# Hybrid encoder trunk on one core: four of sixteen k-tiles of two products as plain float32, and two tiles padded

## The chip, the cores and the metric

The kernel runs on one core of one Trainium2 chip. The metric is the device time of one execution in microseconds (us); before the change it is 3089.78 us, the median of three runs (3088.32 to 3091.51).

## What is computed

The trunk has two layers on 256 tokens of 2048 features, in float32. What matters of the reference:

```python
for i in range(DEPTH):                          # 2
    hn = rmsnorm(h, mix_norm[i])
    if i == 0:
        mix = conformer_conv_module(hn, ...)    # u = hn @ w_pw1 (2048 -> 4096), a * sigmoid(gate),
                                                # 31-tap depthwise convolution, layernorm, silu, @ w_pw2
    else:
        mix = gated_deltanet_bidir(hn, ...)     # proj = hn @ w_in (2048 -> 12416), short convolution,
                                                # two scans over 32 value heads, gated norm, @ w_out
    h = h + mix
    h = h + swiglu_ffn(rmsnorm(h, ffn_norm[i]), w_gate_up[i], w_down[i])   # hidden size 5632
return rmsnorm(h, final_norm)
```

## The kernel before, in words

Features lie on the 128 partitions and the 256 tokens along the free axis. Every product holds a block of 128 output features as its stationary weights and runs over k-tiles of 128 input features. `products` (L163) takes the weights of a column block in chunks of eight k-tiles: one DMA of 512 KB from SP's queue into a tile `raw` (L149), of which there are three. A chunk is cut into groups of four k-tiles.

The matmuls take float32r operands, which hold a float32 less exactly. So `halves` (L152) makes of each group of weights a high part `hi` (a cast on ScalarE, L159) and a low part `lo` (a subtraction on VectorE, L160) that float32r holds exactly, with four buffers of each (`HI`). The activations are split in the same way: `norm_tile` (L213) writes the high part of a k-tile to the left half of a tile `xs` (L219) and the low part to the right half (L220); the residual stream is multiplied by the norm's weights there, and the token's factor comes behind the product. Two forms of product use them:

- *wide* (L184, L185, L187): per k-tile a matmul of 512 columns, `hi` with both halves of the activations, and one of 256 columns, `lo` with the high half. This form is used in pw2 (on `y`), in both SwiGLU stages (`gu` on `xs`, `dn` on `hs`) and in wout (on `ys`).
- *not wide* (L189, L190, L191): three matmuls of 256 columns per k-tile, all added up in one half of a PSUM bank. This form is used in the first product of the convolution module (pw1, 32 blocks of 128 features) and in the input product of the DeltaNet (win, 97 blocks), both with 16 k-tiles on `xs`.

The stages follow each other: pw1 with the taps of the depthwise convolution, on GpSimd (L344), VectorE (L354) and, for four blocks, TensorE (L340); layer norm and pw2; SwiGLU 0; the DeltaNet; wout; SwiGLU 1; the final norm. In the DeltaNet VectorE also works on the short convolution (L594), the inverses (L690 to L730) and the heads (L810), and GpSimd on the masks and inverses. The order of the instructions on each engine is set when the program is built: a scheduler with a model of the times places them, and priorities lift some (`halves` by 800, the heads and the front of the DeltaNet by 550). Each engine works through its own list in that order, and SP's queue too: a load of weights waits there until its `raw` tile is free, and what stands behind it waits as well.

Tiles lie one behind another in a partition, in the order in which the pools are opened: constants (with `par_sb`), activations (`xs`), weights (`raw`, `hi`, `lo`), small tiles, and then the pools of the stages. The starts are multiples of 32 bytes.

Of the kernel before, what the change touches and what calls it, by code (L numbers as in the profile page):

```python
# [7 lines left out]
F32 = mybir.dt.float32  # L8
F32R = mybir.dt.float32r
AF = mybir.ActivationFunctionType  # L10
# [3 lines left out]
P = 128  # L14
# [11 lines left out]
# PSUM banks  # L26
# [11 lines left out]
# taps of the depthwise convolution that GpSimd adds, by feature block  # L38
NPOOL = [15] * 12 + [14, 13, 6, 5]

# columns of the packed per-feature parameters
# [11 lines left out]
# columns of the packed constants  # L53
# [13 lines left out]
def fv(ap, off, *dims):  # L67
    """A view of a tile by an offset and [stride, count] pairs over its free elements."""
    return bass.AP(ap.tensor, ap.offset + off, [list(ap.ap[0]), *[list(d) for d in dims]])


class Trunk:
    def __init__(self, ctx, tc, x, par, cst, pw1, pw2, win, wout, gu, dn, out):
# [15 lines left out]
        self.par = self.cp.tile([P, NRES], F32, name="par_sb")  # L89
# [3 lines left out]
    def new_h(self):  # L93
        """The residual stream on chip, in a pool of its own."""
# [8 lines left out]
    def load_first(self, srcs):  # L103
        """The input and the first weights, in the order in which they are needed."""
# [34 lines left out]

    def raw_tile(self):  # L140
        """A chunk of weights; every other one from a phase that has room for more of them."""
# [4 lines left out]
    def raw_weights(self, src, k0, n):  # L146
        """n k-tiles of one column block."""
# [4 lines left out]
    def halves(self, raw, i, n, pool=None):  # L152
        """k-tiles i to i + n as a high and a low part that float32r holds exactly."""
# [9 lines left out]
    def products(self, srcs, kt, acts, wide=False, tags=("lin",), pool=None, order=None):  # L163
        """Blocks of 128 output features, k-tile by k-tile; acts: float32r tiles [P, hi | lo].

        order: of the k-tiles, within each CS of them."""
# [3 lines left out]
        for k0 in range(0, kt, CK):  # L170
            n = min(CK, kt - k0)
            raws = self.ahead.pop(0) if self.ahead else [self.raw_weights(s, k0, n) for s in srcs]
            for i in range(0, n, CS):
                m = min(CS, n - i)
                ws = [self.halves(r, i, m, pool) for r in raws]
# [31 lines left out]

    def norm_begin(self):
# [4 lines left out]
    def norm_tile(self, k, wname, wi, prep=True, first=None):  # L213
# [3 lines left out]
        if prep:  # L217
# [26 lines left out]
    def warm(self, func, after):  # L244
        """Loads a function's table on ScalarE, ahead of its use."""
        t = self.sp.tile([P, 1], F32, tag="warm", bufs=1, name=self.nm("warm"))
        self.nc.scalar.activation(t, after[:, :1], func)
# [10 lines left out]
    def norm_end(self):  # L258
        """The factor is traced behind the next product, whose result is the first to need it."""
# [4 lines left out]

    def conv_module(self, next_norm):
# [3 lines left out]
        with tc.tile_pool(name="conv", bufs=1, reuse_waits="tile") as cv:  # L269
            self.norm_begin()  # L270
# [26 lines left out]
            def add(key, t, n, last):  # L297
                """Sums over the channels, added up in PSUM."""
# [658 lines left out]
```

## Time and profile before

| | |
|---|---|
| median of three runs | 3089.78 us |
| lowest and highest run | 3088.32, 3091.51 us |
| span of the profiled execution | 3092.0 us |
| TensorE matmul busy | 2859.3 us (92%), x18122 |
| VectorE busy | 2332.2 us (75%), x3735 |
| ScalarE busy | 1695.6 us (55%), x3449 |
| GpSimd busy | 1009.9 us (33%), x1047 |
| mean granted clock of TensorE | 0.970 |
| stages, by the first and last of their work, us | pw1 5 to 314, pw2 348 to 440, SwiGLU 0 440 to 1183, DeltaNet 1183 to 2132, wout 2132 to 2336, SwiGLU 1 2336 to 3078 |

The profile is of one execution. Its span is the time from the first to the last instruction; no time of its own is given for that execution beside the span, which is 2.2 us above the median and 0.5 us above the slowest run. PE is TensorE's matmul, PEld its weight load, DVE VectorE, ACT ScalarE, POOL GpSimd and SP the engine that issues most DMAs. The end of a matmul is modelled, and matmuls overlap: how fast they follow each other is read from their starts. The granted clock is TensorE's, as a share of 2.4 GHz.

### The profile page before, as it was taken

The numbers are of one execution on the slowest core, as the hardware profiler recorded it, in microseconds if no ns is written. First come the engines' busy times: TensorE is split into PE (matmuls) and PEld (weight loads), VectorE is DVE, ScalarE is ACT, GpSimd is POOL, SyncE is SP. The second block draws the span as 40 slices with busy tenths as digits, with TensorE's granted clock in tenths as the row PEclk, the third lists the DMA queues.
The fourth block names the chain that finished last, engine by engine and source line by source line (L and its number), as shares of the span: only waits on it lengthen the run. The fifth ranks groups of instructions, "written<-read, shape, count | busy, mean of one in ns | idle before, by whom it ended". The sixth has DMA issues, their size and how long they took to land. (4 is left out here: it accounts for less than half of the span.)

```text
span 3092.0 us, 50294 instructions
## 1 busy us (share of the span) xinstructions
PE 2859.3 (92%) x18122; PEld 2566.7 (83%) x18122; DVE 2332.2 (75%) x3735; ACT 1695.6 (55%) x3449; POOL 1009.9 (33%) x1047
## 2 busy tenths in 40 slices
PE   7778799999999999878888889888999999999998
PEld 6777688888888889877888888888888888888887
DVE  8999876666666667899899997985766666666555
ACT  6665555555555445654665456554545555555443
POOL 6777420000000111566667766562110000000111
PEclk9999899999999999999999999999999999999999
DMA  4333266555556665543544445456666555556664
GB/s 164 121 112 103 89 202 189 188 185 188 186 186 193 197 200 166 181 150 115 164 155 149 137 144 166 129 158 200 192 189 209 185 187 188 185 187 184 192 190 141
DMA packets 163866, 521.38 MB, mean 169 GB/s; under 512 B 18240, under 2 KB 34944, under 8 KB 163616
## 3 DMA queue, kind: packets, MB, share of 16 engines
q1 hardware_dynamic: 162320, 516.86, 52.7%
q8 instruction: 142, 2.33, 0.3%
q10 hardware_dynamic: 1296, 1.30, 0.1%
q14 instruction: 108, 0.88, 0.1%
HBM read 497.02 MB, written 21.07 MB: 168 GB/s over the span
## 5 line engine op out<-in xcount | busy, mean ns | idle before, releaser
L160 DVE TENSOR_TENSOR lo<-raw,hi 128x512 fp32r<-128x512 f32 x1764 | 1384.7, 788 | 644.6 <-ACT hi L159 638.3
L159 ACT CAST hi<-raw 128x512 fp32r<-128x512 f32 x1764 | 1085.9, 619 | 935.4 <-PE acc L185 692.8
L185 PE MATMUL acc<-xs,hi 128*128 128x512 f32 x2816 | 982.0, 398 | 0.6 <-ACT hi L159 0.6
L184 PE MATMUL acc<-xs,lo 128*128 128x256 f32 x2640 | 742.3, 281 | 0.0
L191 PE MATMUL acc<-xs,lo 128*128 128x256 f32 x2064 | 620.1, 302 | 96.4 <-DVE lo L160 95.6
L189 PE MATMUL acc<-xs,hi 128*128 128x256 f32 x2064 | 606.1, 295 | 31.1 <-ACT hi L159 18.9
L185 PEld LDWEIGHTS acc<-xs,hi 128*128 128x128 f32 x2816 | 517.7, 188 | 116.4 <-ACT hi L159 0.9
L190 PE MATMUL acc<-xs,hi 128*128 128x256 f32 x2064 | 605.2, 294 | 0.8 <-DVE xs L220 0.7
L191 PEld LDWEIGHTS acc<-xs,lo 128*128 128x128 f32 x2064 | 410.9, 200 | 128.8 <-DVE lo L160 123.0
L184 PEld LDWEIGHTS acc<-xs,lo 128*128 128x128 f32 x2640 | 499.0, 189 | 6.8
L185 PE MATMUL acc<-hs,hi 128*128 128x512 f32 x1408 | 486.8, 391 | 0.0
L189 PEld LDWEIGHTS acc<-xs,hi 128*128 128x128 f32 x2064 | 413.8, 201 | 37.1 <-ACT hi L159 21.1
L190 PEld LDWEIGHTS acc<-xs,hi 128*128 128x128 f32 x2064 | 413.9, 201 | 6.1 <-issue 4.3
L184 PE MATMUL acc<-hs,lo 128*128 128x256 f32 x1376 | 388.0, 282 | 0.0
L421 POOL TENSOR_TENSOR tg<-tg,rstd 128x256 f32<-128x256 f32 x88 | 65.0, 738 | 920.9 <-ACT tg L420 920.9
L185 PEld LDWEIGHTS acc<-hs,hi 128*128 128x128 f32 x1408 | 262.2, 188 | 53.4
L184 PEld LDWEIGHTS acc<-hs,lo 128*128 128x128 f32 x1376 | 259.9, 189 | 1.6
L230 POOL TENSOR_TENSOR sq<-h 128x256 f32<-128x256 f32 x59 | 55.0, 931 | 562.7 <-DVE h L432 383.9
L344 POOL TENSOR_TENSOR a<-a,m 128x256 f32<-128x256 f32 x218 | 196.3, 908 | 56.1 <-ACT m L343 45.8
L594 DVE SCALAR_TENSOR_TENSOR u<-t,par_sb,u 128x254 f32<-128x254 f32 (+1 forms) x256 | 178.8, 704 | 3.4 <-ACT u L590 2.2
L185 PE MATMUL acc<-ys,hi 128*128 128x512 f32 x512 | 177.8, 396 | 1.1 <-DVE ys L204 1.1
L184 PE MATMUL acc<-ys,lo 128*128 128x256 f32 x496 | 137.9, 286 | 1.8 <-ACT ys L203 1.6
(226 smaller groups left out, 3503.9 us busy)
## 6 DMA issues: line engine op xcount, KB each, us to landing
raw<-in_gu SPq DMA_DIRECT2D x352, 512.0 KB, 4.6
raw<-in_win SPq DMA_DIRECT2D x194, 512.0 KB, 3.8
raw<-in_dn SPq DMA_DIRECT2D x160, 512.0 KB, 3.6
raw<-in_pw SPq DMA_DIRECT2D x94, 512.0 KB, 3.3
raw<-in_wout SPq DMA_DIRECT2D x64, 512.0 KB, 3.7
a_d<-am SPq DMA_DIRECT2D x32, 384.0 KB, 2.7
ar<-a_d SPq DMA_DIRECT2D x32, 384.0 KB, 4.8
raw<-in_dn SPq DMA_DIRECT2D x32, 256.0 KB, 4.3
```

Source lines behind the costliest of these rows:

```text
L159: nc.scalar.copy(hi, r)
L160: nc.vector.tensor_tensor(lo, r, hi.bitcast(F32), op=ALU.subtract)
L184: nc.tensor.matmul(acc[:, S:], lo, a[:, :S], start=False, stop=False)
L185: nc.tensor.matmul(acc, hi, a, start=first, stop=last)
L189: nc.tensor.matmul(acc[:, :S], hi, a[:, :S], start=first, stop=False)
L190: nc.tensor.matmul(acc[:, :S], hi, a[:, S:], start=False, stop=False)
L191: nc.tensor.matmul(acc[:, :S], lo, a[:, :S], start=False, stop=last)
L230: (nc.vector if last else nc.gpsimd).tensor_tensor(sq, h, h, op=ALU.mult)
L344: nc.gpsimd.tensor_tensor(acc, acc, m, op=ALU.add)
L421: nc.gpsimd.tensor_tensor(tg, tg, rstd, op=ALU.mult)
L594: nc.vector.scalar_tensor_tensor(u[:, lo:hi], t[:, lo + s : hi + s], w(i), u[:, lo:hi], op0=ALU.mult, op1=ALU.add)
```

## The change

In the products on the norm's output, a norm may now name groups of k-tiles as *plain*: group 0 for pw1 (`PLAIN1`), group 3 for win (`PLAIN2`, passed by SwiGLU 0, whose last norm feeds the DeltaNet). For such a group `norm_tile` writes the product of the residual stream with the norm's weights as float32, without a low part, and `products` multiplies the loaded weights as they are: one plain float32 matmul of 256 columns per k-tile in place of three, with `raw` itself as the stationary operand and no cast and no subtraction. Besides, `par_sb` is padded from 499 to 512 columns and `warm` from 1 to 32. Comments are blanked as well; with the added lines, what stands behind them moves down by up to 16.

```diff
+PLAIN1, PLAIN2 = (0,), (3,)
...
-        self.par = self.cp.tile([P, NRES], F32, name="par_sb")
+        self.par = self.cp.tile([P, -(-NRES // 32) * 32], F32, name="par_sb")[:, :NRES]
...
                 m = min(CS, n - i)
+                if acts[order[k0 + i]].dtype == F32:
+                    for x in range(k0 + i, k0 + i + m):
+                        for acc, r in zip(accs, raws):
+                            nc.tensor.matmul(acc[:, :S], r[:, (x - k0) * P : (x - k0 + 1) * P], acts[order[x]],
+                                             start=(x == 0), stop=(x == kt - 1))
+                    continue
                 ws = [self.halves(r, i, m, pool) for r in raws]
...
-    def norm_begin(self):
+    def norm_begin(self, plain=()):
+        self.plain = plain
...
-        if prep:
+        if prep and k // CS in self.plain:
+            xs = self.xp.tile([P, 2 * S], F32, tag=f"xs{k}", name=self.nm(f"xp{k}"))[:, :S]
+            nc.scalar.activation(xs, h, AF.Copy, scale=w)
+            self.xs[k] = xs
+        elif prep:
...
-        t = self.sp.tile([P, 1], F32, tag="warm", bufs=1, name=self.nm("warm"))
-        self.nc.scalar.activation(t, after[:, :1], func)
+        t = self.sp.tile([P, 32], F32, tag="warm", bufs=1, name=self.nm("warm"))
+        self.nc.scalar.activation(t[:, :1], after[:, :1], func)
...
-            self.norm_begin()
+            self.norm_begin(PLAIN1)
...
-            self.norm_begin()
+            self.norm_begin(PLAIN2 if prep else ())
```

How this stands in the built programs. On TensorE, at the end of the third block of the DeltaNet's input product, the kernel before has (a row is line, operation, result, moving operand and weights, size; the numbers tell buffers apart):

```order
L189 MATMUL acc_2650_12874<-xs14_2565_12403,hi_2659_12927 128x256
L190 MATMUL acc_2650_12874<-xs14_2565_12403,hi_2659_12927 128x256
L191 MATMUL acc_2650_12874<-xs14_2565_12403,lo_2660_12928 128x256
L189 MATMUL acc_2650_12874<-xs15_2596_12557,hi_2659_12927 128x256
L190 MATMUL acc_2650_12874<-xs15_2596_12557,hi_2659_12927 128x256
L191 MATMUL acc_2650_12874<-xs15_2596_12557,lo_2660_12928 128x256
L189 MATMUL acc_2666_12958<-xs0_2132_10249,hi_2668_12961 128x256
```

and the changed kernel, at the end of that block:

```order
L199 MATMUL acc_2582_12458<-xs11_2408_11553,hi_2589_12495 128x256
L200 MATMUL acc_2582_12458<-xs11_2408_11553,hi_2589_12495 128x256
L201 MATMUL acc_2582_12458<-xs11_2408_11553,lo_2590_12496 128x256
L182 MATMUL acc_2582_12458<-xp12_2439_11707,raw_2588_12493 128x256
L182 MATMUL acc_2582_12458<-xp13_2470_11860,raw_2588_12493 128x256
L182 MATMUL acc_2582_12458<-xp14_2501_12013,raw_2588_12493 128x256
L182 MATMUL acc_2582_12458<-xp15_2532_12166,raw_2588_12493 128x256
L199 MATMUL acc_2596_12530<-xs0_2068_9861,hi_2598_12533 128x256
```

The last four k-tiles are four rows in place of twelve, and they read `raw` instead of `hi` and `lo`. On VectorE, where the same blocks' weights are split at the start of the DeltaNet, the kernel before has four subtractions for the third block (those from raw_2651 and raw_2656):

```order
L160 TENSOR_TENSOR lo_2653_12878<-raw_2651_12875,hi_2652_12877 128x512
L255 RECIPROCAL rstd_2619_12735<-rstd_2619_12735 128x256
L160 TENSOR_TENSOR lo_2655_12894<-raw_2651_12875,hi_2654_12893 128x512
L535 TENSOR_TENSOR t_2620_12738<-acc_2607_12664,rstd_2619_12735 128x256
L160 TENSOR_TENSOR lo_2658_12912<-raw_2656_12909,hi_2657_12911 128x512
L589 TENSOR_TENSOR t_2645_12859<-acc_2634_12790,rstd_2619_12735 128x256
L536 TENSOR_SCALAR t_2620_12738<-t_2620_12738,cst_sb_70,par_sb_71 128x256
L160 TENSOR_TENSOR lo_2660_12928<-raw_2656_12909,hi_2659_12927 128x512
```

and the changed kernel three (from raw_2583 and raw_2588):

```order
L163 TENSOR_TENSOR lo_2585_12462<-raw_2583_12459,hi_2584_12461 128x512
L163 TENSOR_TENSOR lo_2587_12478<-raw_2583_12459,hi_2586_12477 128x512
L271 RECIPROCAL rstd_2553_12331<-rstd_2553_12331 128x256
L163 TENSOR_TENSOR lo_2590_12496<-raw_2588_12493,hi_2589_12495 128x512
L551 TENSOR_TENSOR t_2554_12334<-acc_2543_12272,rstd_2553_12331 128x256
L552 TENSOR_SCALAR t_2554_12334<-t_2554_12334,cst_sb_70,par_sb_71 128x256
L163 TENSOR_TENSOR lo_2599_12534<-raw_2597_12531,hi_2598_12533 128x512
```

The subtraction for the fourth group is gone, and the next one in the list is that of the next block. In all, the program has 1635 subtractions of weights for 1764 before, as many casts less, 56 subtractions of `xs` for 64, and 516 plain matmuls in place of 1548.

## Rows read from the trace of the kernel before

**Rows 1.** The page: the span and part 1, busy us, share, number of instructions.
```profile
span 3092.0 us, 50294 instructions
...
PE 2859.3 (92%) x18122; PEld 2566.7 (83%) x18122; DVE 2332.2 (75%) x3735; ACT 1695.6 (55%) x3449; POOL 1009.9 (33%) x1047
```
**Rows 2.** Busy time by stage: the stretch, its length, then as the first row says.
```profile
core 0: us, PE busy (x) PEld busy (x) DVE busy (x) ACT busy (x) POOL busy (x), PEclk, DMA share, GB/s
45.00:305.00 260.00, 200.92 (x1358) 180.84 (x1357) 255.30 (x349) 161.59 (x347) 197.84 (x222) 0.95 0.33 108
...
440.00:939.00 499.00, 498.20 (x2822) 432.24 (x2821) 320.39 (x574) 281.21 (x531) 34.22 (x46) 1.00 0.59 189
939.00:1183.00 244.00, 244.00 (x1408) 215.94 (x1407) 151.67 (x224) 117.57 (x193) 28.81 (x31) 1.00 0.64 193
1183.00:2132.00 949.00, 829.34 (x6361) 787.45 (x6360) 857.40 (x1341) 529.61 (x1255) 573.06 (x507) 0.94 0.48 154
...
2336.00:2833.00 497.00, 497.00 (x2818) 431.57 (x2817) 319.56 (x573) 280.85 (x530) 34.20 (x46) 1.00 0.59 189
```
**Rows 3.** Groups, 45:305, DVE: tiles, shapes, count; busy us, mean ns; idle before.
```profile
L160 DVE TENSOR_TENSOR lo<-raw,hi 128x512 fp32r<-128x512 f32 x109 | 106.1, 980 | 0.0
```
**Rows 4.** The same view, 440:939, two groups of two engines.
```profile
L185 PE MATMUL acc<-xs,hi 128*128 128x512 f32 x1408 | 491.1, 398 | 0.6 <-ACT hi L159 0.6
...
L160 DVE TENSOR_TENSOR lo<-raw,hi 128x512 fp32r<-128x512 f32 x353 | 244.3, 693 | 172.1 <-ACT hi L159 171.9
```
**Rows 5.** Timeline of PE in the DeltaNet, nine matmuls apart: start us, us.
```profile
1191.58 0.28 PE L191 MATMUL acc<-xs,lo 128*128 128x256 f32 x1
...
1192.65 0.28 PE L191 MATMUL acc<-xs,lo 128*128 128x256 f32 x1
```
**Rows 6.** Groups, whole span, PE: the taps' matmuls.
```profile
L340 PE MATMUL taps<-up,diag 128*128 128x256 f32 x96 | 25.1, 415 | 8.4 <-DVE up L330 5.7 <-DVE b L357 2.7
```
**Rows 7.** Timeline of PE in pw1: ten records of the taps and what follows.
```profile
256.64 2.32 PE L340 MATMUL taps<-up,diag 128*128 128x256 f32 x10
258.80 0.59 PE L302 MATMUL s<-a,cst_sb 128*128 128x256 f32 x2
```
**Rows 8.** Groups, 1183:2132, DVE.
```profile
L160 DVE TENSOR_TENSOR lo<-raw,hi 128x512 fp32r<-128x512 f32 x387 | 372.5, 969 | 46.2 <-ACT hi L159 44.8 <-PE acc L191 0.2
```
**Rows 9.** Waits, 1183:2132, PE: waiter <- waited for: us, times, longest.
```profile
PE acc L191 <- DVE lo L160: 44.2, 32, 4.8
PE psb L804 <- DVE rx L810: 18.2, 9, 3.9
PE acc L189 <- ACT hi L159: 8.5, 4, 3.9
PE acc L189 <- DVE t L589: 8.1, 4, 3.3
```
**Rows 10.** Groups, 939:1183, PE.
```profile
L185 PE MATMUL acc<-hs,hi 128*128 128x512 f32 x704 | 243.4, 391 | 0.0
```
**Rows 11.** Timeline of PE in wide products: on xs, on y, on ys.
```profile
699.81 0.40 PE L185 MATMUL acc<-xs,hi 128*128 128x512 f32 x1
...
701.23 0.62 PE L185 MATMUL acc<-xs,hi 128*128 128x512 f32 x2
...
390.10 0.40 PE L185 MATMUL acc<-y,hi 128*128 128x512 f32 x1
...
391.86 0.40 PE L185 MATMUL acc<-y,hi 128*128 128x512 f32 x1
...
2249.75 0.39 PE L185 MATMUL acc<-ys,hi 128*128 128x512 f32 x1
...
2251.13 0.39 PE L185 MATMUL acc<-ys,hi 128*128 128x512 f32 x1
```
**Rows 12.** Waits of SP's queue, whole span.
```profile
SPq L149 <- DVE lo L160: 1748.2, 643, 44.8
```
**Rows 13.** Issues of DMAs, whole span: count, KB each, median us to landing.
```profile
raw<-in_win SPq DMA_DIRECT2D x194, 512.0 KB, 3.8
```

## The prediction

> **What bounds the kernel now.** I read the page first, then the busy time by stage, then the groups by line inside each stage, then the waits, and last the timeline of TensorE for the spacing of its matmuls. The page says that TensorE is busy 92% of a span of 3092.0 us [rows 1]; that share is a mean over two kinds of stage. In both SwiGLU stages PE is busy all the time at the full clock of 2.4 GHz, and VectorE is not [rows 2]. In the first product of the convolution module (45 to 305 us) it is the other way round: DVE is busy 255.3 of 260 us and PE 200.9. In the DeltaNet (1183 to 2132 us) DVE is busy 857 of 949 us, PE 829, and the clock is granted at 0.94 on average, that is, some of the time at 1.2 GHz [rows 2]. So time can be won from DVE in two stages, and from PE's own spacing in the others. The profiled span is 2.2 us above the median of the three runs shown (3089.78); I sum changes and apply them to the median.
>
> **Term 1: the split that goes, in the convolution module.** Each block of 16 k-tiles splits its weights in four groups, each one ACT cast (L159) and one DVE subtraction (L160). The change drops one of the four groups for 32 blocks of pw1 and 97 of win: 129 subtractions. In the window 45:305 DVE runs 109 of them at a mean of 980 ns [rows 3]; a quarter, 27, goes. The same instruction takes 693 ns in the SwiGLU stage, where POOL is busy 34 of 499 us [rows 4]. So 27 x 0.980 = 26 us is the upper end and 27 x 0.693 = 19 us the lower one for a stage that DVE bounds. Below both lies 10 us, if ACT or POOL keeps the taps from moving up; POOL is busy 198 of 260 us [rows 2]. I take **20 us**, near the lower end of the two, because POOL's work stays and stands in a shorter stage.
> The Trainium skill, "SBUF — State Buffer", section on the two separate sides, says that a DVE instruction with two SBUF inputs and a GpSimd instruction that reads SBUF exclude each other for a whole instruction. By that rule the part over 693 ns belongs to POOL's instruction and falls on the next DVE instruction, so term 1 would be 19 us; without it, 26 us. That the mean is longer where POOL is busy agrees; which share moves on, no row shows.
>
> **What is put on PE.** A k-tile of those products is three float32r matmuls of 256 columns now. Nine of them in a row take 1192.65 - 1191.58 = 1.07 us [rows 5], 0.357 us a k-tile. A plain float32 matmul leaves two records: the 48 tap matmuls of L340 are x96 in the trace [rows 6]. Ten such records of 256 columns take 258.80 - 256.64 = 2.16 us [rows 7], so 0.432 us a k-tile: 0.075 us more, 0.30 us a block. In pw1 that is 32 x 0.30 = 10 us, in a stage where PE is idle for 59 of 260 us [rows 2]: I cost it at nothing, and if that cover is gone it takes half of term 1.
>
> **Term 2: the DeltaNet.** Here neither end is near. If DVE set the whole time, 97 x 0.969 [rows 8] = 94 us would go. If PE set it, nothing would go and 97 x 0.30 = 29 us would come. I go by PE's account of the 949 us, of which it is idle 120. It waits 44.2 us for lo and 8.5 for hi, and 18.2 + 8.1 for two other results of DVE [rows 9]. A quarter of the splits goes, DVE's load falls from 90% to about 83%, and each block now ends (see the order) in 1.7 us of matmuls that wait for no split, in which DVE can run ahead. I take three quarters of the first two waits, 40 us, and a third of the others, 9 us. The clock at 0.94 costs 6% of 949, 57 us; PE's clock falls after idle time, idle falls by 49 of 120, and I count half of that share, 12 us. Less the 29 us that come: **32 us** gained. It is nearer the middle of +29 and -94 because DVE and PE come out about level: PE's 829 + 29 - 12 = 846 us against DVE's 857 - 67 (97 x 0.693) = 790.
>
> **Term 3: the padding.** par_sb goes from 499 to 512 columns and warm from 1 to 32. In the built programs xs, raw, hi and lo then start at multiples of 128 B in a partition; before, they start 96 B behind one (xs0 at 22752, now 22784). hs (111872) and ys (109824) start at multiples of 128 B in the kernel before, y of pw2 (171712) is 64 B behind one. The wide product of 16 k-tiles on xs, 1408 k-tiles, takes 499 and 497 us; the one on hs, 704 k-tiles of the same two matmuls with the same weights' buffers, takes 244 [rows 2]. Four times that is 976, so the two on xs are 20 us longer, to the 1 us or so by which the windows are cut. The mean record of its 512-column matmul is 398 ns against 391 [rows 4, 10]. From the timeline a k-tile is 355 ns on xs (four in 1.42 us), 352 on y (five in 1.76), 345 on ys (four in 1.38) [rows 11]: the slow ones are those that start off a multiple of 128 B. I take nearly all of it, **18 us**. Ends: 0, and some 22 if weights that start evenly help too; no row has float32r weights and operand both even, so I exclude neither.
>
> **Costed at nothing.** ACT loses 129 casts; it is busy 530 of 949 us there [rows 2]. Eight xs subtractions (L220) go: four at the start, four beside a stretch where DVE is busy 152 of 244 us [rows 2].
>
> **Sum:** 20 + 32 + 18 = 70 us. 3092.0 becomes 3022, and the median of 3089.8 becomes **3020 us**.
>
> **The rivals.**
> *A, padding does nothing (0.20).* The longer stage on xs has another cause than the place: blocks of 16 k-tiles where hs has blocks of 44, one evacuation more often. For it: the stages differ in that as well. Against it: the timelines are taken inside blocks, and y, 64 B off with blocks of 16, lies between. Term 3 is 0, and the time 3038. The Trainium skill, "SBUF — State Buffer", specifications, gives SBUF cachelines of 16 bytes; by that rule a shift of 32 B moves nothing onto or off a line, and the time would be 3038 too. The rows on y and ys so far speak against it.
> *B, DVE alone bounds the DeltaNet (0.12).* All of its stretches with DVE at 100% shrink and PE's 29 us hide in PE's idle time: 857/949 of 94 us, 85 us in place of 32. Time 3090 - 20 - 85 - 18 = 2967. For it: DVE's 90%. Against it: PE's waits for lo are 44 us, not 120.
> *C, PE takes over in the DeltaNet (0.11).* The waits that go are just paid back by the longer matmuls; term 2 is 0 and the time 3052. For it: the first 70 us of the stage already run with PE full, and there plain tiles only cost.
> *D, slower: the weights arrive late (0.05).* A raw tile was free once its two subtractions were done; SP's queue waited for just that, 643 times [rows 12]. Now a tile with a plain group stays taken until PE's last plain matmul, and there are three tiles. In the DeltaNet the two loads of block b+2 start at the end of block b: two loads in a row at 3.8 us [rows 13], then a cast and a subtraction (about 1.6 us), a split group (1.4 us) and the plain group (1.7 us) make 12.3 us for two blocks, 6.2 us each, under the 9.8 us (949/97) that a block takes. It decides from loads of (19.6 - 4.7)/2 = 7.4 us on, if the queue holds them up so long behind other waits. At 8.2 us a block would take 10.6: +78 us, and with terms 1 and 3 the time is 3130. Against it: the landing times are half of that.
> That the change does not do what it says is out: the order has 1635 subtractions instead of 1764 and 516 plain matmuls.
>
> **How the numbers follow.** The forecast has the other 0.52, with a range of its own of 3000 to 3037 (DeltaNet 20 to 50 us, term 1 from 15 to 26). The range of 2968 to 3062 takes in A, C and nearly all of B's upper half, and leaves out D and the rest of B, with the case where little of any term comes: about 0.18. A measurement of this kernel can tell some 0.2%, 6 us, from no change. Faster: 0.52 + 0.20 + 0.12 + 0.11 less 0.02 for a C in which padding fails and term 1 is small: 0.93. Within 0.2%: 0.02. Slower: D, 0.05.
>
> **What would show it.** Right: the pw1 stage ends about 20 us sooner, with DVE still near 100%; the DeltaNet takes some 917 us with PE's wait for lo near 10 us and the clock above 0.94; plain records of 256 columns follow each other at 216 ns; both wide products on xs take about 488 us, at 346 ns a k-tile. Wrong: those products still take 498 us (A); a DeltaNet under 880 us (B), or of 940 and more with PE full (C); casts or plain matmuls that wait for the raw DMA for tens of us (D).

## The result and the profile after

The changed kernel takes 3108.81 us (median of four runs, 3102.23 to 3110.02), the kernel before beside it 3090.65 us (four runs, 3088.32 to 3092.26). The ratio is 1.0046, with a 95% interval of 1.0034 to 1.0058: slower by 14 us (10 to 18 by the interval), half a percent but clear of noise, where 70 us of gain were forecast. The profiled execution took 3109.0 us, with a span of 3107.2. First the page of the changed kernel, to be held against [rows 1]:

```profile
span 3107.2 us, 48822 instructions
...
PE 2889.0 (93%) x17606; PEld 2564.0 (83%) x17606; DVE 2213.8 (71%) x3598; ACT 1615.9 (52%) x3320; POOL 980.0 (32%) x1047
```

DVE lost 118 us of work and ACT 80, as the edit says; PE gained 30 us with 516 records less; and the span grew by 15.2. Next the busy time by stage (columns as in [rows 2]):

```profile
45.00:305.00 260.00, 205.22 (x1246) 184.97 (x1245) 238.95 (x329) 153.41 (x334) 206.92 (x235) 0.94 0.31 106
...
934.00:1181.00 247.00, 247.00 (x1411) 216.45 (x1410) 149.83 (x222) 117.67 (x194) 28.61 (x31) 1.00 0.65 191
1181.00:2150.00 969.00, 853.59 (x6003) 786.38 (x6002) 775.01 (x1257) 473.18 (x1177) 548.29 (x507) 0.95 0.46 153
2347.00:2845.00 498.00, 498.00 (x2824) 432.56 (x2823) 320.80 (x574) 280.56 (x531) 34.10 (x46) 1.00 0.58 189
```

In the first row, the first product of the convolution module (pw1), DVE is busy 238.95 of 260 us, no longer 255.30. The DeltaNet is 20 us longer (969 us for 949) although DVE is busy 775 us there, no longer 857. The down product of SwiGLU 0 takes 247 us, no longer 244, with PE full in both. The wide product on xs is where it was.

To compare runs stage by stage, this case uses the last starts of the wide products, which mark the ends of the stages to within one matmul. In this view of a line of the matmuls (count: shortest, median, longest ns; first and last start in us) they are the numbers behind "to"; of the kernel before and of the changed one:

```profile
L185 PE MATMUL acc<-hs,hi x704: 390/390/399, 938.6 to 1182.8; 128*128 128x512 f32 x176
L185 PE MATMUL acc<-ys,hi x512: 390/390/792, 2132.1 to 2335.2; 128*128 128x512 f32 x171
L185 PE MATMUL acc<-y,hi x256: 389/394/793, 347.7 to 439.8; 128*128 128x512 f32 x128
```

```profile
L195 PE MATMUL acc<-hs,hi x704: 387/396/401, 933.6 to 1180.4; 128*128 128x512 f32 x176
L195 PE MATMUL acc<-ys,hi x512: 387/396/797, 2149.6 to 2347.2; 128*128 128x512 f32 x171
L195 PE MATMUL acc<-y,hi x256: 387/396/796, 343.8 to 435.7; 128*128 128x512 f32 x128
```

The part up to pw2's end got 4.1 us shorter (439.8 to 435.7). From the end of SwiGLU 0 to the end of wout it was 2335.2 - 1182.8 = 1152.4 us and is 2347.2 - 1180.4 = 1166.8: +14.4. (DeltaNet and wout go together, because a later start of wout makes it shorter.) The two down products add 2.7 us each, gate and up gives back 1.0. The same cuts for every kernel of this study, in us of its profiled execution:

| kernel | to the end of pw2 | gate and up, 0 and 1 | down, 0 and 1 | DeltaNet and wout | span |
|---|---|---|---|---|---|
| before | 439.8 | 498.6, 497.3 | 244.4, 244.8 | 1152.4 | 3092.0 |
| changed | 435.7 | 497.7, 497.2 | 247.1, 247.5 | 1166.8 | 3107.2 |
| pad_only | 438.5 | 501.4, 497.3 | 247.1, 247.5 | 1151.5 | 3098.2 |
| relief_only | 425.4 | 497.3, 497.3 | 244.4, 244.8 | 1126.7 | 3050.6 |
| price_only | 449.3 | 497.3, 497.3 | 244.4, 244.8 | 1181.1 | 3128.9 |
| hold_only | 439.1 | 498.6, 497.3 | 244.4, 244.8 | 1171.8 | 3110.7 |
| no_hold | 435.5 | 498.6, 497.3 | 244.4, 244.8 | 1155.3 | 3090.5 |
| after_nopad | 436.3 | 498.0, 498.3 | 244.4, 244.8 | 1167.9 | 3105.0 |
| before_fine | 437.9 | 497.2, 497.3 | 244.4, 244.8 | 1163.1 | 3099.4 |
| after_fine | 433.5 | 497.2, 497.2 | 247.1, 247.5 | 1157.9 | 3095.4 |
| conv_fine | 431.7 | 497.2, 497.3 | 244.4, 244.8 | 1166.6 | 3096.8 |
| place224 | 437.3 | 490.6, 490.3 | 244.4, 244.8 | 1153.3 | 3075.6 |
| place128 | 440.7 | 494.9, 493.3 | 244.4, 244.8 | 1149.4 | 3082.4 |
| fine_place | 431.1 | 490.3, 490.3 | 244.4, 244.8 | 1155.6 | 3071.4 |

How far a number carries: before, pad_only, place224 and place128 have the same code up to pw2 and in the DeltaNet, and lie within 3.4 us (437.3 to 440.7) and 4 us (1149.4 to 1153.3). Each row is one execution: those of after_nopad and after_fine took 5.1 and 5.9 us more than the medians of their kernels, the other kernels' lie within 1.5 us of theirs, and the span of the kernel before lies 1.3 us above the median of its times.

**Where the wait went.** The waits in the DeltaNet (waiter <- waited for: us, times, longest), to be held against [rows 9]. First the casts' wait for the weights and one wait of PE in the kernel before:

```profile
ACT hi L159 <- DMA raw<-in_win: 12.5, 10, 2.6
...
PE pssum L613 <- ACT th L612: 6.0, 4, 2.3
```

and in the changed kernel, engine by engine; SP is the queue of the loads:

```profile
ACT hi L162 <- DMA raw<-in_win: 173.1, 69, 7.5
...
DVE lo L163 <- ACT hi L162: 95.2, 67, 4.4
```

```profile
PE pssum L629 <- ACT th L628: 30.8, 11, 6.0
PE acc L201 <- DVE lo L163: 12.5, 8, 6.7
...
PE psb L833 <- ACT w2s L827: 12.1, 8, 2.7
PE pssum L859 <- DVE s L618: 10.5, 6, 3.1
```

```profile
SPq L152 <- DVE lo L163: 299.8, 66, 12.3
SPq L152 <- PE acc L182: 90.4, 44, 8.6
```

PE's wait for lo fell from 44.2 to 12.5 us, which is what the prediction asked for. But ACT's casts now wait 173.1 us for the weights' DMA where they waited 12.5, DVE's subtractions wait 95.2 us for those casts (44.8 before, in the idle column of [rows 8]), and PE waits for th and w2s, which share ACT's list with the casts, and for s, which DVE makes from th. SP's queue waits 44 times for a plain matmul (L182) to let a raw tile go, and longer still for subtractions. One of the places where a cast is late, from 2062 to 2074 us, by the timelines of DVE, SP, ACT, DVE again and PE (start, length, instruction, idle time before):

```profile
2063.09 3.33 DVE L163 TENSOR_TENSOR lo<-raw,hi 128x512 fp32r<-128x512 f32 x1
```

```profile
2066.44 0.33 SPq L152 DMA_DIRECT2D raw<-in_win  x1
```

```profile
2070.52 0.62 ACT L162 CAST hi<-raw 128x512 fp32r<-128x512 f32 x1 [7.51 <-DMA raw<-in_win]
2071.04 0.41 ACT L617 ACTIVATE th<-u 128x256 f32<-128x256 f32 x1
```

```profile
2071.17 0.69 DVE L163 TENSOR_TENSOR lo<-raw,hi 128x512 fp32r<-128x512 f32 x1 [1.54 <-ACT hi L162]
...
2072.91 0.41 DVE L618 SCALAR_TENSOR_TENSOR s<-th,u 128x256 f32<-128x256 f32 x1
```

```profile
2069.84 1.03 PE L182 MATMUL acc<-xp,raw 128*128 128x256 f32 x4
2073.47 0.41 PE L859 MATMUL pssum<-cst_sb,s 128*128 128x128 f32 x2 [2.60 <-DVE s L618]
2073.72 1.03 PE L182 MATMUL acc<-xp,raw 128*128 128x256 f32 x4
```

The cast waits 7.51 us for its tile. Behind it stands th (L617), behind th on DVE stands s, and for s PE stops 2.60 us in the middle of a plain group, half of whose matmuls are still to come. So a late tile delays PE. But here it was not a plain matmul that made the tile late: the load left the queue at 2066.44, when a subtraction of 3.33 us had ended (2063.09 + 3.33 = 2066.42), and the cast began 4.1 us later. It is so in most of the DeltaNet. With casts and loads matched by their order (three casts and two loads a block), 148 of the 173 us of waiting fall on loads that a result of DVE had released, and 8 on loads that a plain matmul had released. How a held tile makes the loads late that do not wait for it themselves, the traces do not say; that it does is for the experiments to show.

### The profile page after: what moved, and what is told of

It reads as the page before. It is cut to its first block, busy times and chain, and to the rows that moved or that the text cites. A ratio compares the mean times of both kernels' runs of the same rounds, so it can differ in the third digit from the quotient of the medians.

```text
span 3107.2 us, 48822 instructions
## 1 busy us (share of the span) xinstructions
PE 2889.0 (93%) x17606; PEld 2564.0 (83%) x17606; DVE 2213.8 (71%) x3598; ACT 1615.9 (52%) x3320; POOL 980.0 (32%) x1047
## 5 line engine op out<-in xcount | busy, mean ns | idle before, releaser
L163 DVE TENSOR_TENSOR lo<-raw,hi 128x512 fp32r<-128x512 f32 x1635 | 1243.0, 763 | 726.2 <-ACT hi L162 717.0
L162 ACT CAST hi<-raw 128x512 fp32r<-128x512 f32 x1635 | 1004.7, 619 | 1019.4 <-PE acc L195 696.5
L194 PE MATMUL acc<-xs,lo 128*128 128x256 f32 x2640 | 742.3, 281 | 0.1
L195 PEld LDWEIGHTS acc<-xs,hi 128*128 128x128 f32 x2816 | 517.6, 188 | 115.4
L194 PEld LDWEIGHTS acc<-xs,lo 128*128 128x128 f32 x2640 | 499.0, 189 | 7.3 <-DVE lo L163 0.5
L201 PE MATMUL acc<-xs,lo 128*128 128x256 f32 x1548 | 459.9, 297 | 43.4 <-DVE lo L163 43.2
L199 PE MATMUL acc<-xs,hi 128*128 128x256 f32 x1548 | 478.2, 310 | 10.2 <-ACT hi L162 9.4
L200 PE MATMUL acc<-xs,hi 128*128 128x256 f32 x1548 | 454.0, 294 | 0.2
L201 PEld LDWEIGHTS acc<-xs,lo 128*128 128x128 f32 x1548 | 306.5, 198 | 56.2 <-DVE lo L163 51.1
L199 PEld LDWEIGHTS acc<-xs,hi 128*128 128x128 f32 x1548 | 306.3, 198 | 22.8 <-ACT hi L162 11.0
L200 PEld LDWEIGHTS acc<-xs,hi 128*128 128x128 f32 x1548 | 306.5, 198 | 7.7 <-issue 3.2
L182 PE MATMUL acc<-xp,raw 128*128 128x256 f32 x1032 | 261.4, 392 | 6.8 <-ACT xp L231 4.7
L182 PEld LDWEIGHTS acc<-xp,raw 128*128 128x128 f32 x1032 | 191.6, 198 | 32.2 <-ACT xp L231 5.0
```

The lines of the kernel that those rows point to most:

```text
L162: nc.scalar.copy(hi, r)
L163: nc.vector.tensor_tensor(lo, r, hi.bitcast(F32), op=ALU.subtract)
L182: nc.tensor.matmul(acc[:, :S], r[:, (x - k0) * P : (x - k0 + 1) * P], acts[order[x]], start=(x == 0), stop=(x == kt - 1))
L194: nc.tensor.matmul(acc[:, S:], lo, a[:, :S], start=False, stop=False)
L195: nc.tensor.matmul(acc, hi, a, start=first, stop=last)
L199: nc.tensor.matmul(acc[:, :S], hi, a[:, :S], start=first, stop=False)
```

## The experiments

The edits below are to the kernel before unless said otherwise.

### pad_only: the padding alone

```diff
-        self.par = self.cp.tile([P, NRES], F32, name="par_sb")
+        self.par = self.cp.tile([P, -(-NRES // 32) * 32], F32, name="par_sb")[:, :NRES]
...
-        t = self.sp.tile([P, 1], F32, tag="warm", bufs=1, name=self.nm("warm"))
-        self.nc.scalar.activation(t, after[:, :1], func)
+        t = self.sp.tile([P, 32], F32, tag="warm", bufs=1, name=self.nm("warm"))
+        self.nc.scalar.activation(t[:, :1], after[:, :1], func)
```

> The kernel before with the two padded tiles alone. In the changed kernel the two products on hs take 247.2 and 247.6 us in place of 244.5 and 245.0, and those on xs are unchanged. If the padding makes that, it shows here too: 3.091 to 3.099 ms, the DeltaNet at 949 us within 5. If the plain matmuls change it in some way, the products on hs stay at 245 and the time at 3.088 to 3.093 ms.

3099.38 us for 3092.57, ratio 1.0023 (1.0013 to 1.0032). That is 6.8 us (4 to 10), just past the range that was named for a padding that costs. The wide products on xs are no faster (497.3 us in SwiGLU 1, as before). The down products are slower: 247.1 and 247.5 us for 244.4 and 244.8, the same 5.4 us as in the changed kernel. In gate and up 0 PE also waits 2.0 us for hi, once. Padding costs; term 3 had the wrong sign.

### relief_only: the subtractions that go, without anything in their place

`late` is set where the DeltaNet begins, so k-tiles 0 to 3 of pw1 and 12 to 15 of win are meant. The matmul that read the low part reads the high part once more.

```diff
-            nc.vector.tensor_tensor(lo, r, hi.bitcast(F32), op=ALU.subtract)
+            if part:
+                nc.vector.tensor_tensor(lo, r, hi.bitcast(F32), op=ALU.subtract)
+            else:
+                lo = hi
...
+        skip = -1 if wide else 12 if self.late else 0
...
-                ws = [self.halves(r, i, m, pool) for r in raws]
+                ws = [self.halves(r, i, m, pool, k0 + i != skip) for r in raws]
```

> The kernel before, in which the low part of one group in four (pw1 and win) is not computed and the high part takes its place in the matmul: the product lacks that term. VectorE loses the same 129 subtractions as in the change; TensorE's work, the casts and the time that a raw tile is held stay. Theory 1 (raw tiles held too long give the relief back): the relief itself is worth its price, pw1 -15 to -25 us, DeltaNet -20 to -45, in all 3.025 to 3.060 ms. Theory 2 (TensorE sets the DeltaNet's time): pw1 -15, DeltaNet -10 at most, over 3.062 ms.

3052.16 us, ratio 0.987 (0.9856 to 0.9885). To the end of pw2 14.4 us go (439.8 to 425.4), in DeltaNet and wout 25.7 (1152.4 to 1126.7). The time and the 25.7 lie in theory 1's ranges, the 14.4 just short of its 15 to 25. This is all that the removed subtractions are worth: 40 us, not the 81 that the prediction counted (20 in term 1; 40 + 9 + 12 in term 2). The busy times in the DeltaNet and PE's waits for ACT and DVE are now:

```profile
1167.00:2089.00 922.00, 820.90 (x6363) 779.23 (x6362) 786.15 (x1245) 528.46 (x1255) 555.57 (x507) 0.95 0.49 159
```

```profile
PE acc L195 <- DVE lo L161: 38.4, 34, 4.1
PE acc L193 <- ACT hi L159: 11.9, 6, 2.7
PE pssum L618 <- ACT th L617: 11.3, 7, 3.3
PE psb L809 <- DVE rx L815: 11.1, 6, 4.0
...
PE acc L193 <- DVE t L594: 3.5, 1, 3.5
```

DVE's busy time falls by 857.40 - 786.15 = 71 us, where 97 instructions of 0.969 us [rows 8] would be 94. Most of the rest comes back on other DVE work: the short convolution's 256 instructions u take 773 ns in place of 704, 18 us more in all. The Trainium skill ("SBUF — State Buffer", the section on the two separate sides) says that such a DVE instruction and a GpSimd instruction that reads SBUF exclude each other for a whole instruction. The prediction took from it that the part over 693 ns falls on the next DVE instruction; by that, an estimate, 97 x 0.693 = 67 us go, and the trace's 71 is near it.

And PE's wait for lo, of which the prediction took three quarters away, fell only from 44.2 to 38.4. The waits for rx and t fell by 7.1 and 4.6 us, but those for ACT's hi and th rose by 3.4 and 5.3. In all PE's idle time went from 120 to 101 us (922.00 - 820.90), and its busy time for the same matmuls from 829 to 821, at a granted clock of 0.95 for 0.94.

### price_only: the plain matmuls alone

Casts, subtractions and the release of the raw tiles stay as before; the plain product reads the high parts. The low parts of these groups are made and not used.

```diff
+        plain = -1 if wide else 12 if self.late else 0
...
-                        if wide:
+                        if k0 + i == plain:
+                            nc.tensor.matmul(acc[:, :S], hi.bitcast(F32), a[:, :S].bitcast(F32), start=first, stop=last)
+                        elif wide:
```

> The kernel before, where the same four of 16 k-tiles of pw1 and win are multiplied once as plain float32 of the high parts instead of in three matmuls; the casts and subtractions are still made (the low parts of these groups are not used) and the raw tiles are free as before. This is TensorE's price alone: 0.075 us by 4 by 129, 38.7 us, without relief and without holding. If it lies on the path in both stages (the account: relief -27, holding +17, price +29 makes the +20 of the DeltaNet): DeltaNet +25 to +30, pw1 +5 to +10, in all 3.118 to 3.132 ms. If it hides beside VectorE's work, as I had it for pw1: DeltaNet +5 to +15, pw1 0 to +3, 3.096 to 3.108 ms.

3131.1 us for 3093.81, ratio 1.0121 (1.0106 to 1.0136). DeltaNet and wout: 1181.1 - 1152.4 = +28.7 us, against 97 x 0.30 = 29 of the prediction. To the end of pw2: 449.3 - 439.8 = +9.5, against 32 x 0.30 = 10. So the price was sized rightly, and all of it lies on the path, in both stages: the first of the two cases that were named. The DeltaNet's row shows it:

```profile
1191.00:2172.00 981.00, 857.88 (x5979) 791.53 (x5978) 861.46 (x1349) 529.95 (x1264) 575.81 (x507) 0.95 0.45 150
```

PE is busy 28.5 us more (857.88 for 829.34), and idle 123 us as against 120: none of the idle time took it in here. The size itself can be read in the changed kernel, in the DeltaNet's first blocks:

```profile
1203.37 0.28 PE L201 MATMUL acc<-xs,lo 128*128 128x256 f32 x1
1203.49 1.89 PE L182 MATMUL acc<-xp,raw 128*128 128x256 f32 x8
1205.03 0.47 PE L199 MATMUL acc<-xs,hi 128*128 128x256 f32 x1
1205.34 0.28 PE L200 MATMUL acc<-xs,hi 128*128 128x256 f32 x1
```

Eight records and the next L199 take 1205.34 - 1203.49 = 1.85 us. The L199 alone is 0.12 us (the spacing from 1203.37 to 1203.49), so the plain group takes 1.73, a split one 12 x 0.12 = 1.44: 0.29 us more.

### hold_only: raw tiles that stay taken

A matmul of four rows and four columns reads the raw tile beside each block's last product; its moving operand is zero.

```diff
+                            if last and self.late:
+                                nc.tensor.matmul(acc[:4, :4], raws[0][:, (n - 1) * P : (n - 1) * P + 4], self.zero,
+                                                 start=False, stop=False)
```

> The kernel before, where in the DeltaNet's input product one added matmul of 4 columns by 4, on zeros, reads each block's second raw tile just before the block's last matmul: the tile is held as long as in the change, nothing else is added but some 0.1 us a block on TensorE (10 us at most). Theory 1: the DeltaNet takes 965 us or more, ScalarE's wait for the loads of win is over 100 us (12.5 before, 173 in the change). Theory 2: at most 957 us, and that wait under 40.

3111.97 us, ratio 1.0067 (1.005 to 1.0084); DeltaNet and wout +19.4. The DeltaNet alone takes 966 us (1182 to 2148), as theory 1 has it. ACT's casts wait for the weights 87.9 us, 48 times, less than the 100 that it named:

```profile
ACT hi L159 <- DMA raw<-in_win: 87.9, 48, 6.6
```

But the run does not measure the holding by itself: the small matmul was to cost 0.1 us a block at most and costs 0.317 (spacings around it of 209, 28, 96 and 224 ns, where two of 120 stood), as at the first block's end:

```profile
1188.53 0.28 PE L194 MATMUL acc<-xs,lo 128*128 128x256 f32 x1
1188.74 0.19 PE L192 MATMUL acc<-os,raw 128*4 128x4 f32 x2
1188.87 0.39 PE L194 MATMUL acc<-xs,lo 128*128 128x256 f32 x1
1189.09 0.28 PE L189 MATMUL acc<-xs,hi 128*128 128x256 f32 x1
```

That is up to 31 us on PE, more than the stage lost. It shows that the casts wait longer where tiles are held to the end of a block; what that costs it leaves open.

### after_fine and before_fine: raw tiles half as large

Six tiles of four k-tiles in place of three of eight, so that a plain group holds half as much. First in the changed kernel, then, as its control, in the kernel before.

```diff
-CK = 8
+CK = 4
...
-RAW = 3
+RAW = 6
...
-        raws = [self.raw_tile() for _ in range(2 * len(srcs))]
+        raws = [self.raw_tile() for _ in range(KD // CK * len(srcs))]
...
-        part(CK, 0, CK)
-        self.load_h(self.x, CK, KD)
+        self.load_h(self.x, CS, 2 * CS)
+        part(2 * CS, 0, CS)
+        part(3 * CS, 0, CS)
+        self.load_h(self.x, 2 * CS, KD)
```

> The changed kernel with raw tiles of four k-tiles, six of them, in place of eight and three: the same room, but the tile of a split group is free at once and only that of the plain group is held. Theory 1: ScalarE's wait for the loads of win falls under 60 us, the DeltaNet to 905 to 940 us, pw1 by 5 to 20, the whole to 3.045 to 3.080 ms. Theory 2: DeltaNet 960 to 975 us, the whole 3.100 to 3.112 ms.

> The kernel before with raw tiles of four k-tiles, six of them; the control for the changed kernel with such tiles. If the finer tiles only undo the holding, nothing changes here: DeltaNet 945 to 955 us, the whole 3.086 to 3.097 ms. If they are worth something of their own (earlier loads, the start), it is 5 us or more faster in both, and the holding is worth that much less.

after_fine takes 3091.26 us, ratio 0.9998 (0.9988 to 1.0007), before_fine 3101.64, ratio 1.0024 (1.0013 to 1.0035). The same edit takes 8.9 us off the changed kernel's DeltaNet and wout and puts 10.7 on those of the kernel before. ACT's wait for the weights in after_fine:

```profile
ACT hi L163 <- DMA raw<-in_win: 17.5, 14, 2.7
```

17.5 us for 173.1, with three casts a block in both: the late weights are gone. Neither run came out as named. after_fine lies between the ranges of its two theories, in the time and in the DeltaNet (955 us, 1178 to 2133); before_fine is 5 us past its range. Why the small tiles cost the kernel before 10.7 us was not followed up. It shows that the same work in another list of instructions can differ by that much.

### conv_fine: the change in pw1 alone

The changed kernel with fine tiles, but without plain groups in the DeltaNet and without padding.

```diff
-PLAIN1, PLAIN2 = (0,), (3,)
+PLAIN1, PLAIN2 = (0,), ()
```

> The change in pw1 alone, with raw tiles of four k-tiles and without the padding. By the stages of the run with fine tiles: pw1 and the gap behind it 6 us shorter than before, the DeltaNet as before: 3.082 to 3.089 ms. If plain tiles cost as much as they relieve there, 3.089 to 3.094 ms.

3099.09 us, ratio 1.0019 (1.001 to 1.0029), past both ranges that were named: they did not count what the small tiles cost by themselves. To the end of pw2 it takes 431.7 us, for 437.9 of its control: 6.2 us won there, against -14.4 + 9.5 = -4.9 from the two runs above. Its DeltaNet and wout, whose code is the control's, take 1166.6 us for 1163.1, 3.5 us more, again the 4 us or so by which equal code differs.

### after_nopad and no_hold: the holding, by a difference

after_nopad is the change without its padding. no_hold has the same relief (the subtractions that go) and the same price (the longer matmuls), but makes the casts, so that a raw tile is free once ACT has read it; it leaves out the low parts of the plain groups (`plain` and `late` as above).

```diff
+            if part:
+                nc.vector.tensor_tensor(lo, r, hi.bitcast(F32), op=ALU.subtract)
+            else:
+                lo = hi
...
-                ws = [self.halves(r, i, m, pool) for r in raws]
+                ws = [self.halves(r, i, m, pool, k0 + i != plain) for r in raws]
...
-                        if wide:
+                        if k0 + i == plain:
+                            nc.tensor.matmul(acc[:, :S], hi.bitcast(F32), a[:, :S].bitcast(F32), start=first, stop=last)
+                        elif wide:
```

> The change without its padding: plain k-tiles in pw1 and in the DeltaNet, par and warm as before. If the padding costs what it cost alone (2.7 us in each of the two down stages, by the place of hs against the weights), both come back to 244.5 to 245.0 us, the DeltaNet stays near 969 us, and the time is 3101 to 3105 us against 3108.8 of the whole change. If the padding did something to the raw tiles that the plain products read, the DeltaNet differs by more than 10 us from 969.

> Relief and price without the holding: in the same group of four k-tiles of every pw1 and DeltaNet block the low part is not made, and the group's three products become one plain float32 product of the high part with the activation's high part; the casts are all made, so a raw tile comes free when ScalarE has read it, as in the kernel before. It leaves out the low parts of those groups. No padding. Theory (relief -27, price +29 to +32, holding the rest): the DeltaNet takes 945 to 957 us, ScalarE's casts wait at most 20 us for raw tiles there, and the time is 3083 to 3094 us, some 12 us or more below the change without padding. Rival (nothing is held; relief and price simply don't add up, because both act on the same waits): DeltaNet 962 us or more, time within 5 us of the change without padding.

after_nopad takes 3101.73 us, in the range that was named for it, ratio 1.0027 (1.0014 to 1.0039); no_hold takes 3090.85, ratio 0.9992 (0.9983 to 1.0002), both against 3093.64. The intervals don't meet: the two kernels differ by 10.9 us, with 129 casts more in the faster one. The DeltaNet of no_hold by itself, from the last down product to the first of wout, took 963 us, over the 957 that was named and just over the rival's 962, while the time lies in the theory's range and not within 5 us of after_nopad. Its wout is 192 us, the shortest of all. DeltaNet and wout together are 1155.3 us, against 1152.4 - 25.7 + 28.7 = 1155.4 from relief and price: there the two add up, though so close an agreement is luck where equal code differs by 4 us. after_nopad has 1167.9, 12.6 us more. So the rival falls by the time and by this sum, but its sign in the DeltaNet alone came. That the 11 to 13 us are the price of the holding rests on the casts' waits, which go with it; the two programs also differ in the order of their lists. The casts' waits in no_hold and in after_nopad, and PE's wait for lo in no_hold:

```profile
ACT hi L159 <- DMA raw<-in_win: 12.2, 8, 3.2
```

```profile
ACT hi L162 <- DMA raw<-in_win: 178.2, 72, 7.5
```

```profile
PE acc L197 <- DVE lo L161: 41.6, 33, 4.1
```

With the tiles freed by the casts, the wait for lo is back at 41.6 us, near the 44.2 of before, and the kernel is faster than the changed one with 12.5. A wait of PE that goes is no gain by itself: another can take its place.

### place224 and place128: where xs lies against the weights

pad_only moved xs, raw, hi and lo by the same 32 B, and xs stayed slow; behind the small tiles, hs and ys moved by 96 B more, and hs became slow. So the distance of the moving operand from the weights could be what counts. By the places of the tiles, modulo 256 B (a period that was chosen, not measured), xs - hi is 0 and hs - hi is 32 in the kernel before; in the changed one xs - hi is 0 still, and hs - hi 128. An unused tile ahead of the weights' pool moves hi, lo, raw and all behind them, but not xs: with 224 B (below) xs - hi becomes 32, with 128 B (32 columns for 56) it becomes 128.

```diff
+        self.gap = pool("gap")
         self.wp = pool("weights")
+        self.gap.tile([P, 56], F32, name="gap")
```

> The kernel before with an unused tile of 224 B between xs and the weights' tiles. The padding moved xs, raw, hi and lo by the same 32 B and left the spacing on xs as it was, 354 ns a k-tile, while hs moved by 96 B against the weights and went from 347 to 351 ns. If it is the place of the moving operand against the weights, modulo 256 B, that sets the spacing, xs now stands to the weights as hs does before (32 B): both products on xs fall to 486 to 490 us and the time to 3.068 to 3.078 ms. If it is something else about xs (blocks of 16 k-tiles), they stay at 497 and the time at 3.086 to 3.095 ms.

> The kernel before with an unused tile of 128 B, not 224, ahead of the weights: xs then starts 128 B past a multiple of 256 from the high parts (before: 0; with 224 B: 32). If the time of a wide k-tile goes by that distance (0: 354 ns, 32: 347 ns, 128: 351 ns as hs showed), each gate-and-up stage takes 494 to 496.5 us. Rival: only the distance of exactly 0 is slow; then 490 to 491 us as with 224. Rival: the 224 B worked through something else than the distance; then 497 us as before or any other value.

place224 takes 3077.01 us, ratio 0.9948 (0.9933 to 0.9963), place128 3084.49, ratio 0.9971 (0.996 to 0.9982). The 512-column matmuls of SwiGLU 0 in the changed kernel (on hs), place224 and place128 (on xs), groups of the whole stage (busy us, mean ns), to be held against those on xs of the kernel before [rows 4]:

```profile
L195 PE MATMUL acc<-hs,hi 128*128 128x512 f32 x704 | 246.1, 393 | 0.0
```

```profile
L187 PE MATMUL acc<-xs,hi 128*128 128x512 f32 x1408 | 483.7, 391 | 0.0
```

```profile
L187 PE MATMUL acc<-xs,hi 128*128 128x512 f32 x1408 | 487.8, 394 | 0.0
```

At a distance of 0 the mean is 398 ns, at 128 it is 393 and 394, at 32 it is 391 (as for hs before, [rows 10]). The stages follow: 497 us at 0, 493 to 495 at 128, 490.5 at 32. The time of place224 lies as named; its two stages end just over the 490 that was named, and the second of place128 just under its 494. Three distances, two operands, the same order: it is the distance that goes with the time. xs starts at the same place in the kernel before and in place224, and in the kernel before xs and hs meet weights in the same buffers, so neither start decides by itself. raw, hi and lo were moved together, so which of them counts is not shown, nor why.

### fine_place: the change at its best

after_fine without the padding and with the 224 B tile.

> The best version of the change that the runs so far suggest: raw tiles of four k-tiles (six of them, so a held one is half as large), no padding, and an unused tile of 224 B ahead of the weights. From the runs: 3091.3 of the change with fine tiles, less 5 for the padding, less 14 for the two gate-and-up stages at 490.5 us each: 3072 us (3064 to 3080), against 3077.0 of the kernel before with the 224 B tile alone. If the gains don't add up, because the list of instructions comes out in another order, the DeltaNet is 960 us or more and the time over 3080.

3072.66 us (3069.48 to 3078.31), ratio 0.9931 (0.9915 to 0.9947): faster than both kernels, and by its interval not to be told from place224, in which no matmul was changed. Of the 20.6 us between the spans, 14.0 come from the 224 B in gate and up (2 x 497.3 less 2 x 490.3; the first of the kernel before has 1.3 us more, as some runs have and some have not) and 8.7 from the part up to pw2; DeltaNet and wout, at 1155.6, are 3.2 longer, which is within the 4 us of equal code. The time lies in the range that was named, and the DeltaNet (957 us, 1166 to 2123) under the 960 that was to show a failure.

## Why the prediction was wrong

The terms as predicted and as measured, in us:

| step | predicted | measured | from |
|---|---|---|---|
| term 1, subtractions of pw1 | -20 | -14.4 | relief_only |
| plain matmuls in pw1 | 0 | +9.5 | price_only |
| term 2, what the splits free in the DeltaNet | -61 | -25.7 | relief_only |
| plain matmuls in the DeltaNet | +29 | +28.7 | price_only |
| raw tiles held (rival D) | 0 | +12.6, +0.8 in pw1 | after_nopad less no_hold |
| term 3, padding | -18 | +5.4 | pad_only |
| sum | -70 | +16.9 | span: +15.2 |

**Term 2 failed most.** Its step that failed is the one from PE's waits to time won: three quarters of the waits for lo and hi were to go, a third of two others, 49 us in all. With the subtractions gone and the rest of the work as it was (relief_only), PE's idle time fell by 19 us. The wait for lo fell by 5.8 us, not by 33; the two others fell by 11.7, more than the 9 that were counted; and part of this came back as waits for ACT's hi and th, 8.7 us more. The clock's share was nearly right: PE's busy time fell by 8, of 12. Of the 61 us 25.7 came, with wout. Taking a quarter off one engine moved the wait to another; why lo gave back so little, the runs do not show. Term 1 gave 14.4 of its 20 us, below the 19 of its lower end; what kept the rest was not followed up.

**The price: its size was right, its cover was not.** 0.30 us a block was read from taps of another stage and came out within 0.01 us. But "costed at nothing" in pw1 rested on PE's idle 59 of 260 us, and that idle time took in next to nothing: price_only paid 9.5 of the 10 us there and 28.7 of the 29 in the DeltaNet. The prediction did say that a lost cover would take half of term 1; it took two thirds of what that term turned out to be.

**Rival D came beside the other terms, but not where the prediction had it decide.** The sign that it gave for D, casts that wait for the raw DMA for tens of us, is what came: 173 us, where no_hold and after_fine have 12 and 17.5. The prediction let D decide from loads of 7.4 us on, if the queue held them up so long, and put it aside because loads land in half of that. That step failed: the landing says nothing of the issue. The loads that the casts waited for landed fast enough, with 3.1 to 6.4 us between their issue and the cast; what was late was their issue, on a queue that waits for subtractions more than for plain matmuls. Nor does it show where PE has no work of the heads. There the plain groups of two blocks in a row start at 1203.49 and 1209.53, 6.04 us apart, well under the mean of 9.8, but that is PE's own work (36 x 0.12 + 1.73 = 6.05), and PE is full, as the row of this stretch shows (columns as in [rows 2]):

```profile
1209.53 1.89 PE L182 MATMUL acc<-xp,raw 128*128 128x256 f32 x8
```

```profile
1181.00:1230.00 49.00, 48.51 (x344) 43.99 (x343) 34.75 (x77) 24.28 (x48) 6.96 (x10) 1.00 0.49 161
```

So the cost must arise elsewhere in the stage; by which steps a held tile delays the other loads there stays open. The measured 11 to 13 us are far from the 78 that the rival named. D alone would not have turned the gain that was forecast into a loss; it did so because the other terms had come to nothing.

**Term 3: the grouping of three rows was read as a rule.** The slow rows were on xs, "off a multiple of 128 B"; ys and hs were on one. The runs show that the time goes with the distance from the weights. The padding left that of xs alone and moved that of hs from 32 to 128 B, a slower one. The size of the gain was nearly there: the tile of 224 B won 14.0 us in gate and up, for the 18 that were forecast. Rival A was right that the padding gains nothing, and wrong that it costs nothing. The Trainium skill ("SBUF — State Buffer", specifications) gives lines of 16 bytes. That a shift of 32 B moves nothing onto or off such a line agrees with xs, 497.3 us before and after. hs moved by whole lines too, 128 B, and each down product lost 2.7 us: there the measurement decides, and lines of 16 bytes do not account for it.

**What held:** the plain records follow each other at 216 ns (8 in 1.73 us); DVE and ACT lose the instructions that were counted; the SwiGLU stages do not change but for the places. Of C's sign, a DeltaNet of 940 us and more with PE full, the first half came and the second did not: PE's longer matmuls are paid in full there while it stays idle for 115 of 969 us. With the measured terms relief and price alone come to -14.4 + 9.5 - 25.7 + 28.7 = -1.9 us, and no_hold, which is that kernel, has a span 1.5 us under that of before. That the terms add up so well is in part luck, for each carries up to 4 us of scatter.

## What to carry to other kernels

An engine's idle time is not yet cover: where several engines feed each other through a few buffers, as here, work added to one of them came out in full although it is idle an eighth of the time, and work taken from another was worth a fraction. When an operation that made a copy is skipped, ask who now reads the original and until when: the tile that was freed early is held to the end of the last reader, and loads can come later for it, also those that do not wait for that tile. Before padding anything, look at where operand pairs lie against each other; an unused tile of 224 B won some 16 us here, and the whole change lost 14.

## What was not expected of the hardware

- The time of the 512-column float32r matmul went with the distance of its moving operand from its weights: modulo 256 B, a mean of 398 ns at 0, 393 to 394 at 128, 391 at 32. Other distances were not tried with an edit, and the cause is not shown.
- A matmul of four columns of plain float32 between float32r ones takes 0.317 us of PE's time, more than a plain group of four k-tiles adds (0.29).
- The 97 subtractions that were removed from DVE gave back 71 us of its busy time for 94 us of their own; most of the difference went to other DVE instructions, of which u grew from 704 to 773 ns.
